# RWKV-7 block on one core: small matrix products handed to TensorE with more reckoned slack, the bonus product after its two parts, and parameter vectors transposed as soon as they are loaded

## The chip, the cores and the metric

The kernel runs on one core of a Trainium2 chip. The metric is the device time of one execution in microseconds (us). Three executions of the kernel before took 1826.38, 1829.63 and 1830.56 us; the median is 1829.63 us. One further execution was profiled. It took 1826.64 us, and its profile spans 1824.9 us from the first to the last instruction.

Names of the engines as the profile has them: PE is TensorE (matrix products; PEld is its loading of the stationary operand), DVE is VectorE, ACT is ScalarE, POOL is GpSimd, SP is SyncE, which only issues transfers here (SPq is its queue).

## What is computed

One layer of a decoder block in float32, 1024 positions of width 1024 (the two blocks of 512 positions are called b = 0 and b = 1 below):

```
h = rms_norm(x, norm_mix)
p = h @ w_in                      # 1024 x 5408: r k v | wd ad gd | conv b c x | gates a, b
p_rw = p_rw + (token_shift(p_rw) - p_rw) * mu_shift
out_a = rwkv7(r, k, v, wd, ad, gd, ...)        # 8 heads of 64
out_b = b * conv3(c * x_c)
x = x + (sigmoid(ga) * (out_a @ w_proj_a) + sigmoid(gb) * (out_b @ w_proj_b)) @ w_out_mix
x = x + cross_attention(rms_norm(x), rms_norm(mem))      # 4 heads, 256 memory tokens
x = x + relu(rms_norm(x) @ w_up)**2 @ w_down
y = rms_norm(x)
```

and within `rwkv7`, for each head and position t:

```
log_w = -softplus(-(w0 + tanh(wd) @ w_lora_w)) - 0.5;  decay = exp(-exp(log_w))
a = sigmoid(a0 + ad @ w_lora_a);  g = sigmoid(gd) @ w_lora_g
S_t = S_{t-1} diag(w_t) + (S_{t-1} a_t) b_t^T + v_t k_t^T;   y_t = S_t r_t
y   = group_norm(y) * ln_x_w + ln_x_b
y   = y + sum(r * k * r_k) * v                 # the bonus
out = y * g
```

## The kernel before

**Products in split form.** Every large float32 product is made of three passes over operands split in two parts: hi (the value rounded by ACT to the format that PE reads in one pass) and lo (the rest, subtracted by DVE or POOL). The weights are split on the chip as they come in (`wh`, `wl`), and so are the activations. One pass is a product of 128x128 by 128x512.

**Streams and a planner.** The program's order is not written out. Each piece of work is a Python generator (a stream); `Scheduler` keeps a reckoned time for each engine (`free`), a reckoned end of every write and read of a tile, and takes PE's reckoned time as "now". A stream yields the time from which it may go on. `need(t, ...)` is the reckoned end of the last write to these tiles plus 0.7 us; `pace("DVE")` is DVE's reckoned free time minus 0.3 us. `Scheduler.run` goes through the side streams in a fixed order of rank and takes the first that is ready; only when none is ready does the main stream (the large products) take its next step. So `need(x) + 0.7` in place of `need(x)` means: let PE's reckoned time pass by 0.7 us more, with products of the main stream in between, before this stream's next instructions are handed out. Each engine then works through its own list strictly in the order that came out, and waits at an instruction whose inputs are not there. The reckoned times decide the order alone; nothing of them is left in the program.

**Stages.** The main stream goes through the projections of `h` (`gemm` over `PROJ`: about 43 column tiles of `w_in`, each for both blocks), then the memory's keys and values (`mem_k`, `mem_v`: weights `w_kv`), `merge`, `w_out_mix`, attention, and the two MLP products. At the program's head `x_stage` turns x into the transposed `h` (PE transposes, ACT and DVE write hi and lo) for b = 0, then b = 1.

**RWKV as side streams beside the projections.** The state recurrence is done in 8 windows (pair of heads by block of 512 positions, `ORDER`), each in chunks of 64 positions:

- `lora_side`: the small products with `w_lora_*`, PSUM tag "c".
- `wkv_prepare(w)`: loads r, k, v, decay and a; DVE and ACT make the scaled operands `T1`, `BK`; then in this order on PSUM tag "s" (two banks, taken by `take_s`): sums of squares with `bd1` (128x2), the bonus sum with `bdo` (two passes, one over the hi and one over the lo part of `bs`), the values minus head mean with `cmat`, the chunk products `BK` by `T1` (`pss<-P,P`, 64 rows by 128 columns, two halves q of two banks h each), and two groups of transposes of `BK` (`pss<-ident,P`).
- `wkv_invert(w)`: POOL solves 32x32 triangles (`ex`), two 32x32 product groups follow.
- `wkv_chain(ws)`: for two windows at a time, 8 chunk steps of small products on tag "c" (`psc<-P,P`), with ACT and DVE copies in between.
- `wkv_out(w, a_)`: group norm of y, and the store to `d_y`.

In the profile nearly all instructions carry line 253, that of the recording helper; so the readings go by tiles. `P` is the ring of work tiles, `H` the ring that holds `h`, `wr` a raw weight tile, `st`, `sh`, `sm`, `ex` small rings, `psg`, `pss`, `psc`, `psy` the PSUM tags ("g" has three banks, "s" two, "c" two, "y" one).

Two details on which the change bears. In `wkv_prepare` the bonus stood as

```
yield need(tm_, bs)
split(bs[:, 0], bs[:, 1], sq)     # ACT makes hi, DVE makes lo
yield from take_s()
o = ps("s", [P, TB])
yield need(o)                     # looks at the PSUM bank alone
mm(o[:], cv["bdo"][:], bs[:, 0], True, False)
```

so nothing let the planner's time run until the two parts were reckoned written. And `constants()` waits until `r1` of block 0 is made (the row scale 1/rms), then transposes `vrow`, the 118 rows of small parameter vectors that SP loads with 16 small transfers behind the loads of x, into `vec`, by way of the one bank of tag "y". The main stream's first pair of jobs needs that bank for block 1.

Of the kernel before, what the change touches and what calls it, by code (L numbers as in the profile page):

```python
# [41 lines left out]
class Scheduler:  # L42
# [156 lines left out]
    def need(self, *tiles):  # L199
        return max(self.written(t) for t in tiles) + 0.7  # L200
# [58 lines left out]
def tile_hybrid_block(  # L259
# [74 lines left out]
    need, pace = sch.need, sch.pace  # L334
# [351 lines left out]
    def constants():  # L686
        yield until(("r1", 0))
        yield need(vrow)
        vps = ps("y", [P, P])
        yield need(vps)  # L690
        PE.transpose(vps[:], vrow[:], ident[:])
        yield need(vps)
        DVE.tensor_copy(vec[:], vps[:])
        cv["omu"] = derived("omu", "mu", -1.0, 1.0)
        cv["hw0"] = derived("hw0", "w0", 0.5)
# [52 lines left out]
    def until(*keys):  # L748
        return lambda: all(k in done for k in keys)
# [335 lines left out]
    def lora_side(name, parts, b, dst, fin):  # L1085
        yield until(("x", 1))
        for j in range(4):
            o2 = ps("c", [P, TB])
            yield need(o2) + 1.0
            cs = slice(j * P, (j + 1) * P)  # L1090
            for m, (lw, x_) in enumerate(parts):
                yield need(lw, x_)
                mm(o2[:], lw[:, cs], x_, m == 0, m == len(parts) - 1)
            yield need(o2)
            yield room
            z = sb("st", [P, TB])
            fin(z, o2, j)
            dma(dst[cs, blk(b)], z[:], (name, j, b))
# [121 lines left out]
    open_s = {"n": 0}  # L1220

    def take_s():

        yield lambda: open_s["n"] < BUFS["s"]
        open_s["n"] += 1
# [10 lines left out]
    def wkv_prepare(w):  # L1236
# [58 lines left out]
        o = ps("s", [P, 4, 2])  # L1295
        yield need(o)
        for q in range(4):
# [16 lines left out]
        split(bs[:, 0], bs[:, 1], sq)  # L1314

        yield from take_s()
# [13 lines left out]
        o = ps("s", [P, 4, 2, C])  # L1330
        yield need(o)
        for q in range(4):
# [26 lines left out]
        for q in range(2):  # L1359
            yield need(T1[0], T1[1], BK)  # L1360
            os_ = []
            for h in range(2):
                yield from take_s()
                o = ps("s", [P, 4, 2 * C])
                yield need(o)
                os_.append(o)
            for c in range(4):
                for h in range(2):
                    mm(os_[h][:, c, :], BK[HALF[h], 4 * q + c, :], T1[h][HALF[h], 4 * q + c, :])
            for h in range(2):  # L1370
                yield from evac_products(os_[h], q, h)
# [4 lines left out]
        for q in range(2):  # L1376
            yield from take_s()
            o = ps("s", [P, 4, P])
            yield need(o)
            for c in range(4):  # L1380
                PE.transpose(o[:, c, :], BK[:, 4 * q + c, :], ident[:])
            give_s()
            ACT.activation(BKt[:, 4 * q:4 * q + 4].rearrange("p c h k -> p c (h k)"), o[:], AF.Copy)
# [14 lines left out]
    def wkv_invert(w):  # L1398
# [35 lines left out]
        o = ps("s", [P, NCH, 32])  # L1434
        yield need(o)
        for c in range(NCH):
# [8 lines left out]
        o = ps("s", [P, NCH, 32])  # L1445
        yield need(o)
        for c in range(NCH):
# [7 lines left out]
    def wkv_chain(ws):  # L1455
# [16 lines left out]
        for c in range(NCH):  # L1472
            last = c == NCH - 1
            keep = not last or b == 0
            yield need(*[w["SV"] for w in ws])

# [18 lines left out]
            for h, H, i, w in HW:  # L1495
                if h == 0:
                    ACT.activation(w["SV"][H, c, h, :], o[H, 1, i], AF.Copy, scale=w["d2"][H, c:c + 1])
                else:
                    DVE.tensor_scalar(w["SV"][H, c, h, :], o[H, 1, i], w["d2"][H, c:c + 1], None, op0=ALU.mult)
            yield need(*[w["SV"] for w in ws])  # L1500
            if keep:
# [21 lines left out]
    def wkv_out(w, a_):  # L1523
# [9 lines left out]
        o = ps("s", [P, 4, 2])  # L1533
        yield need(o)
        for i in range(4):
# [9 lines left out]
        o = ps("s", [P, TB])  # L1545
        yield need(o)
        for i in range(4):
# [601 lines left out]
```

## Time and profile before

| | |
|---|---|
| executions | 1826.38, 1829.63, 1830.56 us, median 1829.63 |
| profiled execution | 1826.64 us, span 1824.9 us |
| busy, whole span | PE 96%, PEld 78%, DVE 59%, ACT 38%, POOL 28% |
| head, 0 to 60 us | PE 44.66 of 60 us busy |
| projections with RWKV, 100 to 600 us | PE 469.27 of 500 us busy, DVE 318.63, POOL 264.33, ACT 155.53 |
| end of RWKV, rest of the projections, 600 to 728 us | PE 59.12 of 60 and 68.00 of 68 us |
| memory keys and values, 728 to 775 us | PE 44.04 of 47 us |
| all after, 775 to 1825 us | PE 1031.40 of 1050 us |

How to read it: an interval of PE that is not busy is idle time "before" the instruction that ends it, and the profile names what released that instruction. A row of grouped instructions has the number of instructions, their busy time and mean duration in ns, and then the idle time of the engine just before them with the releasers. Consecutive products overlap in the records, so a product of 128x512 shows 389 ns while the next one starts about 227 ns later. PEclk is the share of full speed that TensorE's clock was granted.

### The profile page before, as it was taken

What the parts mean: (1) busy time and instruction counts of PE and PEld (TensorE: products, weight loads), DVE (VectorE), ACT (ScalarE), POOL (GpSimd) and SP (SyncE); (2) the same over time, 40 slices, a digit from 0 to 9 for tenths busy, and PEclk for the clock granted to TensorE, in tenths of its full rate; (3) what the DMA queues carried; (4) which work ended last, traced back from release to release, by engine and by line L of the source; (5) the groups of instructions that cost most, each with busy time, mean ns of one, the idle gap of its engine ahead of it and who ended that gap; (6) DMA issues with size and microseconds to landing.
All of it is one profiled execution on the core that took longest, in us unless ns stands there. A gap on an engine that the chain in (4) does not pass through costs nothing.

```text
span 1824.9 us, 26662 instructions
## 1 busy us (share of the span) xinstructions
PE 1756.1 (96%) x9914; PEld 1429.7 (78%) x9914; DVE 1078.5 (59%) x1694; ACT 698.2 (38%) x1233; POOL 518.3 (28%) x872
## 2 busy tenths in 40 slices
PE   7898999999989999999999999989999999999998
PEld 5677767767768788888888877868888888888887
DVE  4477665666754432455556765577767675654543
ACT  5623332123235332422333434354444444543542
POOL 3026653655545110000323433433233220000000
PEclk8999998999999999999999999999999999999999
DMA  6543532323435344744755668434454569765441
GB/s 215 207 125 91 155 93 76 93 82 104 108 86 153 116 139 135 217 162 166 229 179 164 203 190 260 134 102 158 157 178 144 173 196 352 259 213 193 159 118 55
DMA packets 303359, 289.19 MB, mean 158 GB/s; under 512 B 40744, under 2 KB 223134, under 8 KB 303230
## 3 DMA queue, kind: packets, MB, share of 16 engines
q1 hardware_dynamic: 302158, 286.97, 49.3%
q8 instruction: 78, 1.28, 0.3%
q10 hardware_dynamic: 1072, 0.53, 0.1%
q14 instruction: 51, 0.42, 0.1%
HBM read 193.06 MB, written 94.37 MB: 158 GB/s over the span
## 4 chain that ended last, share of the span: by engine, by line
PE 71%; DVE 8%; POOL 5%; issue 3%; DMA 3%; ACT 3%; SPq 0%; POOLq 0%; DVEq 0%; ACTq 0%
PE psg L253 47%; PE pss L253 12%; PE psc L253 9%; DVE P L253 4%; POOL ex L253 4%; PE psy L253 3%; DMA wr<-in_w_kv_dram 2%; ACT P L253 1%; DVE wl L253 1%; DVE st L253 1%; POOL P L253 1%; DVE sh L253 1%; ACT wh L253 1%; DMA P<-dn 0%; SPq L253 0%
## 5 line engine op out<-in xcount | busy, mean ns | idle before, releaser
L253 PE MATMUL psg<-H,wh 128*128 128x512 f32 x1808 | 583.5, 400 | 4.1 <-ACT H L253 1.8
L253 PEld LDWEIGHTS psg<-H,wh 128*128 128x128 f32 x1808 | 338.4, 190 | 75.8 <-ACT H L253 3.1
L253 PE MATMUL psg<-P,wh 128*128 128x512 f32 (+1 forms) x1240 | 371.0, 380 | 7.4 <-ACT P L253 3.0
L253 PE MATMUL psg<-H,wl 128*128 128x512 f32 x888 | 355.4, 400 | 0.0
L253 PEld LDWEIGHTS psg<-P,wh 128*128 128x128 f32 x1240 | 227.9, 188 | 51.7 <-ACT P L253 3.4
L253 PE MATMUL psg<-P,wl 128*128 128x512 f32 (+1 forms) x620 | 235.6, 380 | 0.0
L253 ACT ACTIVATE wh<-wr 128x1024 fp32r<-128x1024 f32 (+2 forms) x187 | 137.8, 764 | 244.3 <-PE psg L253 136.8
L253 DVE TENSOR_TENSOR wl<-wr,wh 128x1024 fp32r<-128x1024 f32 (+2 forms) x178 | 160.2, 923 | 91.4 <-ACT wh L253 90.5
L253 PEld LDWEIGHTS psg<-H,wl 128*128 128x128 f32 x888 | 168.7, 190 | 34.6 <-issue 0.2
L253 ACT ACTIVATE P<-P 128x512 fp32r<-128x512 f32 (+3 forms) x246 | 147.7, 634 | 79.3 <-DVE P L253 44.9
L253 DVE TENSOR_TENSOR P<-P,P 128x512 fp32r<-128x512 f32 (+2 forms) x204 | 146.6, 755 | 14.6 <-ACT P L253 13.2
L253 POOL TENSOR_TENSOR sm<-sm,mhalf 128x8 f32<-128x8 f32 (+2 forms) x18 | 22.8, 1267 | 413.9 <-DVE sm L253 413.9
L253 PEld LDWEIGHTS psg<-P,wl 128*128 128x128 f32 x620 | 116.8, 188 | 21.7 <-DVE wl L253 0.5
L253 POOL TENSOR_TENSOR ex<-ex,P 128x60 f32<-128x60 f32 (+24 forms) x248 | 94.8, 382 | 73.6 <-DMA P<-dn 58.1
L253 POOL TENSOR_TENSOR ex<-ex 128x60 f32<-128x60 f32 (+24 forms) x248 | 98.4, 397 | 19.4
L253 PE MATMUL pss<-P,wh 128*128 128x512 f32 x296 | 91.7, 390 | 1.1 <-DVE P L253 1.1
L253 DVE TENSOR_SCALAR P<-psc,sm 64x64 f32<-64x64 f32 x120 | 34.9, 291 | 88.9 <-ACT P L253 82.4
L253 ACT ACTIVATE P<-psc,sm 64x64 f32<-64x64 f32 (+1 forms) x128 | 42.5, 333 | 100.2 <-PE psc L253 60.1
L253 PE MATMUL psc<-P,P 128*64 128x64 f32 (+2 forms) x816 | 68.1, 252 | 10.3 <-DVE P L253 8.4
L253 DVE TENSOR_TENSOR P<-psg,P 128x512 f32<-128x512 f32 x44 | 30.3, 689 | 78.0 <-PE psg L253 73.7
L253 PEld LDWEIGHTS psc<-P,P 128*64 128x64 f32 (+2 forms) x816 | 46.4, 147 | 37.1 <-issue 15.4
L253 PE MATMUL psc<-P,wh 128*128 128x512 f32 x216 | 67.4, 394 | 0.0
(686 smaller groups left out, 2828.1 us busy)
## 6 DMA issues: line engine op xcount, KB each, us to landing
P<-d_t SPq DMA_DIRECT2D x56, 512.0 KB
wr<-in_w_in_dram SPq DMA_DIRECT2D x40, 512.0 KB
d_t<-P SPq DMA_DIRECT2D x64, 256.0 KB
d_x<-P SPq DMA_DIRECT2D x48, 256.0 KB
P<-d_x SPq DMA_DIRECT2D x24, 512.0 KB
d_t<-st SPq DMA_DIRECT2D x48, 256.0 KB
d_tg<-st SPq DMA_DIRECT2D x32, 256.0 KB
wr<-in_w_kv_dram SPq DMA_DIRECT2D x16, 512.0 KB
```

The lines of the kernel that those rows point to most:

```text
L253: return fn(*args, **kw)
```

## The change

All edits concern when the planner hands out work; no instruction is added or removed, and 8660 PE instructions stand in both programs.

- `constants()`: the transpose of `vrow` no longer waits for `r1`; it is handed out once the fourth tile of `h` of block 0 is made and `vrow`'s transfers are reckoned done, plus 1.0 us. The derived constants still wait for `r1`.
- `lora_side`: 1.5 us more before each of its products.
- `LATE = 0.7` us more before each group of small products of `wkv_prepare`, `wkv_invert` and `wkv_out` (in the chunk products also 1.4 us after the operands), 0.2 us at two points of each chain step.
- The bonus: `need(bs) + LATE` after the split, so that the two passes are handed out when both parts are reckoned written.

```diff
     def constants():
-        yield until(("r1", 0))
-        yield need(vrow)
+        yield until(("h", 0, 3))
+        yield need(vrow) + 1.0
         vps = ps("y", [P, P])
         yield need(vps)
         PE.transpose(vps[:], vrow[:], ident[:])
         yield need(vps)
         DVE.tensor_copy(vec[:], vps[:])
+        yield until(("r1", 0))
...
     def lora_side(name, parts, b, dst, fin):
...
             for m, (lw, x_) in enumerate(parts):
-                yield need(lw, x_)
+                yield need(lw, x_) + 1.5
                 mm(o2[:], lw[:, cs], x_, m == 0, m == len(parts) - 1)
...
+    LATE = 0.7
...
     def wkv_prepare(w):
...
         o = ps("s", [P, 4, 2])
-        yield need(o)
+        yield need(o) + LATE
         for q in range(4):
             mm(o[:, q, :], sq[:, q * P:(q + 1) * P], cv["bd1"][:])
...
         yield need(tm_, bs)
         split(bs[:, 0], bs[:, 1], sq)
-
+        yield need(bs) + LATE
         yield from take_s()
         o = ps("s", [P, TB])
         yield need(o)
...
         o = ps("s", [P, 4, 2, C])
-        yield need(o)
+        yield need(o) + LATE
         for q in range(4):
             mm(o[:, q], v[:, q * P:(q + 1) * P], cv["cmat"][:].rearrange("p h k -> p (h k)"))
...
         for q in range(2):
-            yield need(T1[0], T1[1], BK)
+            yield need(T1[0], T1[1], BK) + 2 * LATE
             os_ = []
             for h in range(2):
                 yield from take_s()
                 o = ps("s", [P, 4, 2 * C])
-                yield need(o)
+                yield need(o) + LATE
                 os_.append(o)
...
             o = ps("s", [P, 4, P])
-            yield need(o)
+            yield need(o) + LATE
             for c in range(4):
                 PE.transpose(o[:, c, :], BK[:, 4 * q + c, :], ident[:])
...
     def wkv_invert(w):
...
         o = ps("s", [P, NCH, 32])
-        yield need(o)
+        yield need(o) + LATE
...
     def wkv_chain(ws):
...
-            yield need(*[w["SV"] for w in ws])
+            yield need(*[w["SV"] for w in ws]) + 0.2
             o = ps("c", [P, 3, 2, C])
...
-            yield need(*[w["SV"] for w in ws])
+            yield need(*[w["SV"] for w in ws]) + 0.2
             if keep:
...
     def wkv_out(w, a_):
...
         o = ps("s", [P, 4, 2])
-        yield need(o)
+        yield need(o) + LATE
...
         o = ps("s", [P, TB])
-        yield need(o)
+        yield need(o) + LATE
```

What moves, at three places.

PE's list at the program's head: `psg` rows are the main stream's first two jobs for block 0 (`H` is `h`), `pss` and `psc` rows with `P_98` the transposes of x for block 1; `psy<-ident,st` is the transpose of the parameter vectors. Before, and then now:

```order
L253 MATMUL psg_196<-H_167,wh_188 128x512
L253 MATMUL psg_196<-H_175,wh_188 128x512
L253 MATMUL psg_196<-H_167,wl_189 128x512
L253 MATMUL psy_390<-ident,st_106 128x128
L253 MATMUL psg_398<-H_160,wh_186 128x512
```

```order
L253 MATMUL psg_196<-H_162,wh_188 128x512
L253 MATMUL psg_196<-H_170,wh_188 128x512
L253 MATMUL psy_281<-ident,st_106 128x128
L253 MATMUL psg_196<-H_162,wl_189 128x512
L253 MATMUL psg_195<-H_163,wh_186 128x512
L253 MATMUL psg_195<-H_171,wh_186 128x512
```

The transpose stood behind the last product of block 0 (eight tiles of `h`); it now stands within the third tile, ahead of five tiles' products and ahead of all transposes of block 1. On DVE the copy to `vec` moves with it: it stood behind the first tiles of block 1, and now stands ahead of the seventh tile of block 0 (`H_174`).

PE's list around the bonus product of the fourth window (`bdo`), in the first chain's time: `psc` and `psy` rows are chain products, `psg` the main stream. Before, and then now:

```order
L253 MATMUL psc_2563<-P_1039,P_914 64x64 x2
L253 MATMUL psc_2563<-P_1486,P_1282 64x64 x2
L253 MATMUL psg_2620<-H_160,wh_2369 128x512
L253 MATMUL psg_2620<-H_168,wh_2369 128x512
L253 MATMUL pss_2625<-P_2599,bdo 128x512 x2
L253 MATMUL psc_2631<-P_1039,P_912 64x64
```

```order
L253 MATMUL psg_2562<-H_167,wl_2333 128x512
L253 MATMUL psg_2690<-H_160,wh_2332 128x512
L253 MATMUL psg_2690<-H_168,wh_2332 128x512
L253 MATMUL psc_2644<-P_1056,P_914 64x64 x2
L253 MATMUL psc_2644<-P_1525,P_1302 64x64 x2
L253 MATMUL pss_2703<-P_2635,bdo 128x512 x2
L253 MATMUL psg_2690<-H_160,wl_2333 128x512
L253 MATMUL psg_2690<-H_161,wh_2332 128x512
```

Counted over the whole list, 754 products of the projections stood ahead of this bonus product, and now 778 do; five products of the projections now stand between it and the next chain step, where none stood.

SP's list where RWKV's last outputs (`sh<-d_y`, with the gate rows `sh<-d_g`) are loaded back for the merge, among stores of gate rows (`d_tg`) and loads of weights (`wr`). Before, and then now:

```order
L253 DMA sh_6572<-d_y 128x512
L253 DMA sh_6574<-d_g 128x512
L253 DMA d_tg<-st_6586 128x512
L253 DMA sh_6609<-d_y 128x512
L253 DMA sh_6611<-d_g 128x512
L253 DMA wr_6632<-in_w_in_dram 128x8x128
L253 DMA d_tg<-st_6625 128x512
L253 DMA d_tg<-st_6660 128x512
L253 DMA wr_6699<-in_w_kv_dram 128x8x128
L253 DMA d_tg<-st_6692 128x512
L253 DMA d_tg<-st_6724 128x512
L253 DMA wr_6763<-in_w_kv_dram 128x8x128
```

```order
L253 DMA d_y<-P_4981 128x512
L253 DMA wr_6673<-in_w_kv_dram 128x8x128
L253 DMA d_tg<-st_6666 128x512
L253 DMA sh_6692<-d_y 128x512
L253 DMA sh_6694<-d_g 128x512
L253 DMA d_tg<-st_6705 128x512
L253 DMA sh_6730<-d_y 128x512
L253 DMA sh_6732<-d_g 128x512
L253 DMA wr_6753<-in_w_kv_dram 128x8x128
L253 DMA d_tg<-st_6746 128x512
L253 DMA sh_6776<-d_y 128x512
L253 DMA sh_6778<-d_g 128x512
```

The first two `w_kv` loads stood behind all `d_y` loads; they now stand among the last three of them. RWKV's last products (the transposes in `wkv_out` of the eighth window) stood behind 1759 products of the projections and now stand behind 1883. From the product that PE started at 685.4 us in the profile before, PE's list is the same to the end.

More of the change, by code (lines that the diff above doesn't have):

```diff
@@ L1545, in wkv_out @@
         o = ps("s", [P, TB])
-        yield need(o)
+        yield need(o) + LATE
         for i in range(4):
```

## The prediction

> **What bounds the kernel now.** I read the busy shares first, then a table by stage, then who ended PE's idle time in the stage that the change touches, then that stage's PE groups with shapes kept apart.
>
> ```profile
> PE 1756.1 (96%) x9914; PEld 1429.7 (78%) x9914; DVE 1078.5 (59%) x1694; ACT 698.2 (38%) x1233; POOL 518.3 (28%) x872
> 100.00:600.00 500.00, 469.27 (x3578) 366.85 (x3578) 318.63 (x587) 155.53 (x304) 264.33 (x648) 0.97 0.38 106
> 600.00:660.00 60.00, 59.12 (x582) 43.22 (x580) 25.03 (x57) 25.25 (x59) 9.35 (x6) 1.00 0.30 89
> 728.00:775.00 47.00, 44.04 (x347) 42.12 (x346) 19.59 (x56) 22.59 (x69) 0.00 (x0) 1.00 0.72 220
> ```
>
> PE is the bound: 96% of the span. The second row and those below are stages: length, busy time of PE, PEld, DVE, ACT and POOL, granted clock, DMA share, GB/s. What small edits can win is PE's idle time and time at a lower clock. Between 100 and 600 us, where RWKV runs beside the projections, PE idles 500 - 469.3 = 30.7 us, and a clock of 0.97 is 0.03 x 500 = 15 us lost. So some 46 us is the ceiling there. DVE, the next engine, is 64% busy in it. Before 660 us the last chains leave PE hardly idle, and from the product at 685.4 us on PE's list does not change.
>
> ```profile
> PE pss L253 <- DVE P L253: 19.0, 19, 3.3
> PE psc L253 <- DVE P L253: 5.2, 9, 1.2
> PE pss L253 <- ACT P L253: 5.1, 4, 1.9
> L253 PE MATMUL pss<-P,P 64*128 64x128 f32 x256 | 27.0, 320 | 13.5 <-DVE P L253 13.2 <-POOL ex L253 0.3
> L253 PE MATMUL pss<-P,bdo 128*128 128x512 f32 x16 | 7.4, 473 | 9.0 <-ACT P L253 5.1 <-DVE P L253 3.8
> L253 PE MATMUL psc<-P,P 128*64 128x64 f32 x472 | 28.9, 243 | 5.4 <-DVE P L253 4.5
> L253 PE MATMUL pss<-ident,P 128*128 128x128 f32 x104 | 16.8, 276 | 2.2 <-DVE P L253 2.0
> L253 PE MATMUL psc<-P,P 128*128 128x512 f32 x24 | 7.7, 415 | 0.7 <-DVE P L253 0.7
> ```
>
> The first three rows are total idle us, times and longest; the others give idle time behind the second bar. All of it but a trace stands ahead of small products that were put into PE's list before DVE or ACT had their inputs: 13.5 + 9.0 + 5.4 + 2.2 + 0.7 = 30.8 us, the whole 30.7. None stands ahead of a large product (the `psg` rows of this stage have 0.0). So PE has other work at these points; it is only queued behind. The critical chain shows how fast that work goes:
>
> ```profile
> 657.64 42.42 PE psg L253 x187
> ```
>
> 42.42 / 187 = 0.227 us for a product of the main stream.
>
> **The change, part by part.** The profiled execution took 1826.6 us; the sum is made against it.
>
> *Bonus, 9.0 us in 8 windows.* One window in full:
>
> ```profile
> 156.71 0.40 PE L253 MATMUL pss<-P,bdo 128*128 128x512 f32 x1
> 157.88 0.80 DVE L253 TENSOR_TENSOR P<-P,P 128x512 fp32r<-128x512 f32 x1
> 158.73 0.50 PE L253 MATMUL pss<-P,bdo 128*128 128x512 f32 x1 [1.63 <-DVE P L253]
> ```
>
> The second pass waits until DVE has written the lo part. With the pass handed out when both parts are reckoned done and 0.7 us more, PE spends that time on main products instead: 1.63 us is seven of them. Bounds: all 9.0 us gone, or nothing if the wait moves on (below). I take 8.0, since two engines must be late by more than 0.7 us against the reckoning for a rest. **-8.0**.
>
> *Chunk products, 13.5 us.* Ten waits; five make nearly all of it:
>
> ```profile
> 167.83 0.58 PE L253 MATMUL pss<-P,P 64*128 64x128 f32 x2 [2.94 <-DVE P L253]
> 280.57 0.80 PE L253 MATMUL pss<-P,P 64*128 64x128 f32 x4 [1.78 <-DVE P L253]
> 354.08 0.38 PE L253 MATMUL pss<-P,P 64*128 64x128 f32 x2 [2.04 <-DVE P L253]
> 403.39 0.58 PE L253 MATMUL pss<-P,P 64*128 64x128 f32 x2 [1.77 <-DVE P L253]
> 525.99 0.47 PE L253 MATMUL pss<-P,P 64*128 64x128 f32 x2 [3.29 <-DVE P L253]
> ```
>
> They wait for the second PSUM bank, from which DVE is still copying the values product. Here only slack is added, 0.7 us on the bank (the 1.4 us on the operands counts only where these are last). The five lose 0.7 each, 3.5 us; the other five, 13.5 - 11.8 = 1.7 us together, go. That is 5.2. With 1.4 it would be 7.0 + 1.7 = 8.7; with a DVE that stays as far behind, 0. I take the lower of the two gains. **-5.2**.
>
> *Chain steps, 5.4 us.* 0.2 us at each of two points. The row above has nine waits of DVE in `psc`, one the 0.7 of `lora_side`; eight lose 0.2 each, 1.6, and what is below that, 5.4 - 4.5 = 0.9, goes. **-2.5**, between 0 and 5.4.
>
> *Transposes of `BK` and `lora_side`, 2.2 + 0.7 us.* Their waits are 0.7 us and less, the slack 0.7 and 1.5. **-2.4**, between 0 and 2.9.
>
> *The parameter vectors, at the head.* What goes is the wait of the bank of tag "y" for `vec`; what comes is a wait for the transfers:
>
> ```profile
> 18.41 0.39 PE L253 MATMUL psg<-H,wl 128*128 128x512 f32 x1
> 21.86 0.29 SPq L253 DMA_DIRECT2D st<-in_norm_final_dram  x1
> 22.03 0.30 PE L253 MATMUL pss<-ident,P 128*128 128x128 f32 x1 [0.72 <-issue]
> 23.33 0.30 PE L253 MATMUL pss<-ident,P 128*128 128x128 f32 x1 [1.00 <-DVE sm L253]
> 35.37 1.22 PE L253 MATMUL psy<-H,wh 128*128 128x512 f32 x2 [2.16 <-DVE vec L253]
> 0.79 0.58 ACTq L253 DMA_DIRECT2D st<-in_norm_mix_dram  x1
> 2.32 0.24 PE L253 MATMUL psy<-ident,st 8*128 8x8 f32 x1 [2.32 <-DMA st<-in_norm_mix_dram]
> ```
>
> The transpose now stands just ahead of the product that started at 18.41, but the last of the 16 small transfers is issued only at 21.86. The first transfer of this kind took from 0.79 to 2.32, 1.5 us, so the rows are there at about 23.4. PE stands still for 23.4 - 18.4 = 5.0 us, with all products of block 0 from the third tile on and all transposes of block 1 queued behind it, and DVE stands before the copy to `vec` with two tiles of `h` behind. 1.7 us (0.72 + 1.00) stood there anyway, since PE now finds those inputs ready; 2.16 goes later: 5.0 - 1.7 - 2.2 = +1.1. Block 1 pays or hides it:
>
> ```profile
> 43.74 0.69 ACT L253 ACTIVATE H<-pss,gmix 128x512 fp32r<-128x512 f32 x1 [5.68 <-PE pss L253]
> ```
>
> ACT idled 5.68 us for block 1's second transposes, which stood behind products of the main stream; they now stand ahead of most of these. Bounds: the two waits gone and nothing for it, -3.9, up to 5.0 and a slice of 3.4 us at half clock behind it, +6.7. I take the difference, **+1.1**.
>
> *Clock.* 15 us of clock went with 30.7 us idle. The slices in which it fell are those of the long waits:
>
> ```profile
> 280.00:300.00 20.00, 18.65 (x194) 14.20 (x194) 10.15 (x24) 5.32 (x16) 0.19 (x1) 0.83 0.22 50
> 400.00:420.00 20.00, 17.14 (x171) 12.76 (x166) 12.84 (x29) 5.21 (x15) 2.51 (x8) 0.83 0.13 22
> 440.00:460.00 20.00, 20.00 (x90) 16.55 (x89) 14.31 (x20) 3.55 (x5) 17.59 (x39) 1.00 0.53 157
> ```
>
> With 18.1 of 30.7 us idle gone, 59%, a proportional share is 8.9 us. But the long waits are shortened, not removed, so I take half, **-4.5**, between 0 and -15. The Trainium skill (TensorE: Matmul & The Clock Gate, Part 1: The HAM clock gate) has the clock fall to half after an idle window of about 3.4 us. Here it fell with no single wait above 3.3 us, so the trace shows it sooner than the page; by the page nothing here would depend on these waits and the term would be 0.
>
> *Waits that move on.* DVE gets no faster; where PE arrives earlier, the next small product may wait instead. I take a quarter of 18.1, **+4.5**, between 0 and 18.1.
>
> Sum: -8.0 - 5.2 - 2.5 - 2.4 + 1.1 - 4.5 + 4.5 = -17.0. That makes 1809.6 us of the profiled execution, which ran 3.0 us below the median; against the median **1812.6 us**.
>
> **Rivals.**
>
> 1. *The waits move on.* For it: five chunk products wait for DVE right after the bonus product, so DVE is late as a whole, not one input. Against it: every moved group has main products put ahead of it, and DVE is 64% busy. Bonus and chunk terms would be 0 and the clock would stay: -2.5 - 2.4 + 1.1 = -3.8, 1825.8 us.
> 2. *RWKV becomes late, slower.* Slack adds up along the windows. RWKV's last products move from behind 1759 to behind 1883 main products, 124 x 0.227 = 28 us later against the projections.
>
> ```profile
> 657.04 0.60 PE L253 MATMUL pss<-ident,P 128*128 128x128 f32 x4
> 673.61 0.32 SPq L253 DMA_DIRECT2D sh<-d_y  x1
> 679.79 0.32 SPq L253 DMA_DIRECT2D sh<-d_y  x1
> 692.74 0.38 SPq L253 DMA_DIRECT2D wr<-in_w_kv_dram  x1
> ```
>
> They ended at 657 and now stand where 685 was, 41 us ahead of the memory stage. SP takes the `d_y` loads 6.2 us apart, and three of them now stand among the `w_kv` loads, which had 12.9 us of room. If y came so late that these loads, 3 x 6.2 = 19 us, fell into the stage at 728, which already runs its DMA at 0.72 and waits for weights, each us would cost one. It decides from 13 us beyond the 28; for slower than before it takes 17 more. At 40 us beyond: 1812.6 + 27 = 1839.6 us. Against it: PE's order fixes the 28.
> 3. *The clock comes back in full*, 15 in place of 4.5: 1802.1 us. For it: a slice without idle time, 440 to 460 us, has 1.00. Against it: 12.6 us of waits stay, in the same places.
> 4. *The clock does not come back* (the page's rule; as a mechanism, the low slices have another cause, such as the sparse small products): 1817.1 us. For it: 280 to 300 us fell to 0.83 with only 1.35 us idle inside. Against it: all low slices lie in or just behind a slice with a long wait.
>
> **How the numbers follow.** Forecast 0.57, rival 1 0.17, rival 2 0.06, rival 3 0.10, rival 4 0.10. 0.2%, 3.7 us, is about what a measurement of this kernel can tell from no change: faster is below 1826.0. Forecast, rivals 3 and 4 and half of rival 1 are faster, 0.85; rival 2 and a little of rival 1 slower, 0.08; the rest is the same, 0.07. The range leaves out rival 2, the upper half of rival 1 and the tail of rival 3: 1799 to 1826. Its low end is the forecast with 8.7 in the chunk term, the full clock and no more than that; the likeliest one's own range is 1804 to 1822.
>
> **What would show it.** In the profile after: `pss<-P,bdo` with under 1 us of idle time; `pss<-P,P` 64*128 at about 8 and `psc<-P,P` 128*64 at about 3; PE busy some 483 of 500 us between 100 and 600, at 0.98; `psy<-ident,st` near 23.4 us with 5 us idle ahead of it and no wait for `vec`; the memory stage begun 17 us earlier. I am wrong if the bonus idle reappears ahead of `cmat` or chunk products, or if PE's time at 60 us is later by more than 3.

## The result and the profile after

| | before | after |
|---|---|---|
| executions, us | 1826.38 to 1833.60 (5), median 1829.63 | 1804.86 to 1810.48 (5), median **1807.4** |
| profiled execution | 1826.64, span 1824.9 | 1810.48, span 1808.8 |

The ratio is **0.9888**, 95% interval 0.9867 to 0.9909, so the change is clear of noise; the medians lie 22.2 us apart. The forecast of 1812.6 us is 5.2 us too high, inside its own range (1804 to 1822). The profiled execution of the change is its slowest of five; it lies 16.2 us under the profiled execution before (forecast: 17.0).

The profile after, in the views that the prediction used. First the busy line of the page, then the table by stage (start and end, length, busy us and instructions of PE, PEld, DVE, ACT and POOL, granted clock, DMA share, GB/s):

```profile
PE 1745.7 (97%) x9914; PEld 1423.7 (79%) x9914; DVE 1078.6 (60%) x1694; ACT 696.6 (39%) x1233; POOL 524.4 (29%) x872
```

```profile
0.00:60.00 60.00, 42.85 (x176) 32.95 (x177) 28.24 (x47) 34.28 (x68) 16.50 (x52) 0.90 0.65 215
100.00:600.00 500.00, 477.88 (x3631) 376.00 (x3630) 325.40 (x591) 158.18 (x308) 271.91 (x647) 0.99 0.38 108
711.00:758.00 47.00, 45.63 (x351) 43.61 (x351) 20.22 (x57) 24.14 (x72) 0.00 (x0) 1.00 0.75 230
```

PE idles 22.1 us between 100 and 600 us (30.7 before) and is granted 0.99 of its clock (0.97). The memory stage begins 18 us earlier (its first product at 704.8 us in place of 723.0), and PE idles 1.4 us in it (3.0).

The waits of that stage by releaser (total us, times, longest), then its groups, idle time behind the second bar:

```profile
PE pss L253 <- DVE P L253: 13.3, 13, 2.1
PE psc L253 <- DVE P L253: 5.4, 7, 1.1
```

```profile
L253 PE MATMUL pss<-P,bdo 128*128 128x512 f32 x16 | 5.6, 422 | 1.0 <-DVE P L253 1.0
L253 PE MATMUL pss<-P,P 64*128 64x128 f32 x256 | 23.7, 301 | 10.0 <-DVE P L253 10.0
L253 PE MATMUL psc<-P,P 128*64 128x64 f32 x472 | 27.7, 236 | 5.5 <-DVE P L253 5.4
L253 PE MATMUL pss<-ident,P 128*128 128x128 f32 x102 | 16.3, 275 | 3.5 <-DVE P L253 1.7 <-ACT P L253 1.6
L253 PE MATMUL pss<-P,P 32*32 32x32 f32 x448 | 10.5, 192 | 1.5 <-issue 0.8 <-DVE P L253 0.6
```

The bonus lost 8.0 of its 9.0 us, the chunk products 3.5 of 13.5. The chain steps kept theirs (5.4 before), the transposes gained 1.3 (2.2 before), and the 32x32 products of the inversion wait 1.5 us where they had waited for nothing.

The head, from the timeline of PE (start, length, the idle time and its releaser in brackets):

```profile
24.20 0.45 PE L253 MATMUL psy<-ident,st 128*128 128x128 f32 x1 [3.77 <-DMA st<-in_norm_final_dram]
56.70 0.76 PE L253 MATMUL psc<-P,P 128*128 128x512 f32 x1 [4.46 <-DVE P L253]
```

PE's 240th main product of the projections starts at 102.3 us (100.5 before); 0.8 us of the difference stands there already at the first main product, ahead of any change, so the head costs 1.0 us. It is not the stop for the vectors alone: up to there PE idles 2.7 us more than before, in which the second line above has a part (a product of `lora_side`, whose wait was 2.97 us before), and one cell less of half clock gives 1.7 us back. Comparing the start of the same products from there on: 18.2 us earlier at the end of the projections, 20.3 in the middle of the output product, 16.2 at the end. Behind the projections PE's list is the same in both, so the change is no reason for the last 4 us. They are 1.6 us more idle time and 1.7 us for one more time at half clock, which began at 1071.9 us, right behind a wait of 1.51 us that the kernel before has too (1.50 us, ended at 1090.3, with no half clock behind it). The other runs that have this part unaltered are 0.8 to 3.6 us longer in it than the kernel before, so it is rather the profiled execution before that was quick here.

Time at half clock between 60 and 690 us, summed from the records of the granted clock that begin there, fell from 27.3 us to 10.2. At half clock half of it is lost: 13.7 us before, 5.1 after. PE's idle time in the same stretch went from 32.0 to 24.3 us. Taken between the same two products instead, the 240th and the last of the projections, the 20.0 us by which they come closer are 9.3 us of idle time, 8.5 us of clock, and 2.2 us in the records themselves: from one product's start to the next, with waits and half clock left out, the bonus products take 4.3 us in place of 6.4 and the chunk products 20.9 in place of 22.1.

These are two single executions, and the one before was not a typical one. Each execution's mean granted clock is on record. Its span times what that clock lacks of 1 is its loss to the clock, over the whole span: 21.6 us on average for the kernel before (60 executions), 16.6 us for the change (10). So the clock gave 5.0 us, with a standard error of 1.0. The time without that loss fell from 1805.8 to 1790.9 us on average, so all the rest gave 14.9. The profiled execution before lost 25.5 us to the clock and took 1801.1 us without that loss. Its profile therefore shows too much of the one and too little of the other, and the split into groups, which profiles alone show, is unsure by some 5 us.

### The profile page after: what moved, and what is told of

It is laid out like the page before. It is cut to its first block, busy times and chain, and to the rows that moved or that the text cites. A ratio compares the mean times of both kernels' runs of the same rounds, so it can differ in the third digit from the quotient of the medians.

```text
span 1808.8 us, 26674 instructions
## 1 busy us (share of the span) xinstructions
PE 1745.7 (97%) x9914; PEld 1423.7 (79%) x9914; DVE 1078.6 (60%) x1694; ACT 696.6 (39%) x1233; POOL 524.4 (29%) x872
## 4 chain that ended last, share of the span: by engine, by line
PE 75%; DVE 8%; DMA 5%; POOL 4%; issue 3%; ACT 3%; SPq 1%; ACTq 0%; POOLq 0%; DVEq 0%
PE psg L253 50%; PE pss L253 12%; PE psc L253 9%; DVE P L253 4%; PE psy L253 4%; POOL ex L253 3%; ACT P L253 2%; SPq L253 1%; DVE wl L253 1%; DMA sh<-d_ob 1%; DVE st L253 1%; POOL P L253 1%; DVE sh L253 1%; ACT st L253 1%; DMA P<-dn 1%
## 5 line engine op out<-in xcount | busy, mean ns | idle before, releaser
L253 PEld LDWEIGHTS psg<-P,wl 128*128 128x128 f32 x620 | 116.8, 188 | 21.8 <-DVE wl L253 0.6
L253 DVE TENSOR_SCALAR P<-psc,sm 64x64 f32<-64x64 f32 x120 | 34.9, 291 | 77.9 <-ACT P L253 72.6
```

The lines of the kernel that those rows point to most:

```text
L253: return fn(*args, **kw)
```

## Experiments

Each ran beside the kernel before on one chip. "Idle" and "half clock" below are PE's idle us and the us lost at half clock between 60 and 690 us, worked out from the records of the profiled execution as above. "Last product" is the start of the profiled execution's last PE instruction against before (the change: -16.2). "Clock, all" and "rest, all" are means over all executions of a run, against those of the kernel before beside it: the loss to the clock over the whole span, and the time without that loss. They are sure to about 2 us and 1 us (standard errors).

| run | ratio (95%) | median us | clock, all | rest, all | idle | half clock | last product |
|---|---|---|---|---|---|---|---|
| before | 1 | 1825.75 to 1829.63 | 0 | 0 | 32.0 | 13.7 | 0 |
| the change, again | 0.9881 (0.9864 to 0.9899) | 1807.0 | -5.5 | -16.4 | 24.2 | 3.4 | -20.3 |
| bonus alone | 0.9970 (0.9958 to 0.9983) | 1819.67 | -2.6 | -3.9 | 28.7 | 6.8 | -9.8 |
| all but the bonus | 0.9996 (0.9981 to 1.0011) | 1826.49 | +2.3 | -3.5 | 33.8 | 13.7 | 0.1 |
| bonus and chunk slack | 0.9900 (0.9882 to 0.9917) | 1810.11 | 0.0 | -18.5 | 22.2 | 13.7 | -17.6 |
| change without chain slack | 0.9919 (0.9893 to 0.9945) | 1813.43 | +0.9 | -15.9 | 24.7 | 3.4 | -19.7 |
| change with old vectors | 0.9891 (0.9876 to 0.9907) | 1805.25 | -4.3 | -17.4 | 21.3 | 5.1 | -23.1 |
| change, LATE 1.4 | 0.9879 (0.9861 to 0.9897) | 1801.89 | -3.2 | -20.8 | 20.4 | 5.1 | -21.9 |
| old vectors, LATE 1.4 | 0.9825 (0.9802 to 0.9849) | 1797.59 | -5.6 | -26.4 | 17.3 | 1.7 | -29.0 |
| old vectors, LATE 2.8 | 0.9933 (0.9915 to 0.9952) | 1814.02 | -2.7 | -9.9 | 25.8 | 10.2 | -12.3 |
| old vectors, LATE 4.2 | 0.9983 (0.9970 to 0.9995) | 1823.02 | +6.1 | -9.5 | 21.8 | 8.5 | -6.1 |
| LATE 1.4, vectors 16 places later | 0.9816 (0.9791 to 0.9841) | 1792.76 | -8.6 | -25.2 | 19.5 | 3.4 | -34.9 |

The median of before differs between the chips and hours by 4 us, so runs of different groups are compared by ratios.

### Base for what follows: the change again

> The changed kernel unaltered, as the base for what runs beside it: a ratio of 0.987 to 0.991 to the kernel before, as in the comparison of the change.

0.9881. The result repeats.

### The bonus alone, and all but the bonus

```diff
 # bonus alone: before, with
         split(bs[:, 0], bs[:, 1], sq)
+        yield need(bs) + 0.7
         yield from take_s()
 # all but the bonus: the change, with
         split(bs[:, 0], bs[:, 1], sq)
-        yield need(bs) + LATE
         yield from take_s()
```

> The kernel before with the bonus wait alone (0.7 us after both parts). Theory A, each wait is its own late input: the idle time ahead of the bonus product goes from 9.0 to about 1, the chunk products keep their 13.5 us, and with the clock's share the time falls by 8 to 12 us, to 1818 to 1822 us; PE's idle time between 100 and 600 us is 22 to 23 us. Theory B, DVE is late as a whole and the waits move on: the chunk and cmat products behind it take what the bonus loses, idle time stays at 28 to 31 us and the time at 1826 to 1830 us.

> The changed kernel with the bonus handed out as before: slack and early vectors alone. Theory A: bonus idle time is back at 9 us, the chunk products have about 10, and the time is what is left of the gain, about 10 to 14 us less than before, 1816 to 1820 us. Theory B, the slack only moves waits and the bonus carries all of the gain: idle time between 100 and 600 us about 30 us, 1828 to 1832 us (the head's 1.8 us included).

The groups between 100 and 600 us, with the bonus alone and then with all but the bonus:

```profile
L253 PE MATMUL psc<-P,P 128*64 128x64 f32 x472 | 27.3, 233 | 9.1 <-DVE P L253 7.9
L253 PE MATMUL pss<-P,P 64*128 64x128 f32 x256 | 26.3, 304 | 10.7 <-DVE P L253 9.0 <-POOL ex L253 1.5
L253 PE MATMUL pss<-P,bdo 128*128 128x512 f32 x16 | 5.5, 408 | 1.2 <-DVE P L253 1.2
```

```profile
L253 PE MATMUL pss<-P,P 64*128 64x128 f32 x256 | 24.1, 305 | 7.0 <-DVE P L253 6.8
L253 PE MATMUL pss<-ident,P 128*128 128x128 f32 x92 | 14.4, 275 | 4.8 <-DVE P L253 4.1 <-ACT P L253 0.7
L253 PE MATMUL pss<-P,bdo 128*128 128x512 f32 x16 | 8.8, 550 | 12.8 <-DVE P L253 7.6 <-ACT P L253 5.1
```

The bonus alone comes between the two theories: its wait goes as theory A had it (7.8 us), the chunk products lose 2.8 us too, and of these 10.6 us 4.9 return, 3.7 of them in the chain steps (5.4 to 9.1). The time falls by 0.3%, some 3 to 8 us, less than theory A's 8 to 12. All but the bonus can't be told from before by its time: the chunk products lose 6.5 us, but the bonus product gains 3.8 (9.0 to 12.8) and the transposes gain 2.6. Over all its executions 3.5 us are gained beside the clock and 2.3 are lost to it. So on its own the slack does nearly what rival 1 says: it moves waits. The two edits alone are worth 0.30% and 0.04%, together 1.1 to 1.2%. They don't add, and which of them "carries" the gain has no answer: **the slack pays in full only once the bonus wait, which stood in its way, is gone.** All but the bonus has the early vectors in it, which cost some 1 to 3 us (below); the slack with neither was not run.

### Which slack: the chunk products' alone, and the chain's taken out

```diff
 # bonus and chunk slack: bonus alone, with
-            yield need(T1[0], T1[1], BK)
+            yield need(T1[0], T1[1], BK) + 2 * 0.7
...
-                yield need(o)
+                yield need(o) + 0.7
 # change without chain slack (both places)
-            yield need(*[w["SV"] for w in ws]) + 0.2
+            yield need(*[w["SV"] for w in ws])
```

> The kernel before with the bonus wait and the slack of the chunk products (1.4 us after the operands, 0.7 after each bank), nothing else. The bonus alone took 10 us off the profiled execution, all together 16 to 20. Theory A, the chunk slack is what works only once the bonus wait is gone: chunk idle time falls from 10.7 (bonus alone) to 6 to 8 us, the long waits that are followed by half clock go from four to two or less, ratio 0.989 to 0.992. Theory B, the rest of the slack (chain, bd1, cmat, transposes, inversion, output) is needed as well: 0.995 to 0.998, as with the bonus alone.

> The changed kernel without the 0.2 us at the two points of each chain step. Theory A, the chain slack does nothing (its idle time was 5.4 us before and 5.5 after): the time of the changed kernel within 2 us, chain idle time 5 to 6 us. Theory B, it holds back waits that would have grown, as they did with the bonus alone (9.1 us): chain idle time 8 to 9 us, the time 3 to 5 us above the changed kernel. Theory C, it costs: the time 2 to 4 us below.

The chunk products with the first, then the chain steps and the chunk products without the chain's slack:

```profile
L253 PE MATMUL pss<-P,P 64*128 64x128 f32 x256 | 22.3, 287 | 9.1 <-DVE P L253 6.4 <-POOL ex L253 2.7
```

```profile
L253 PE MATMUL psc<-P,P 128*64 128x64 f32 x492 | 28.1, 231 | 9.3 <-DVE P L253 8.1
L253 PE MATMUL pss<-P,P 64*128 64x128 f32 x256 | 21.7, 287 | 7.6 <-DVE P L253 5.2 <-POOL ex L253 2.1 <-POOL P L253 0.3
```

Bonus and chunk slack bring 0.990, some 18 of the 22 us, as theory A has it for the time. Its picture of why failed: chunk idle time fell by 1.6 us only (10.7 to 9.1), the chain steps lost more (9.1 to 4.1), and the clock gave nothing. Half clock stands in five places where the bonus alone had three, 13.7 us of loss for 6.8, and over all executions the clock loses as much as before (0.0), while the rest gains 18.5.

Without its slack the chain waits 9.3 us in place of 5.5, the 8 to 9 of theory B, and the median is 6.4 us above the change's beside it. The intervals overlap a little, and the profiled execution was the fastest of six, so the price is less sure than the wait. In that execution PE's idle time as a whole is the same with and without the chain's slack (24.2 and 24.7 us); over all executions too the rest is the same (-16.4 and -15.9), and what differs is the clock (-5.5 and +0.9). So the 0.2 us did not take away waits that stood there; they held back those that the other edits would have sent there, and what that is worth seems to lie in the clock.

### More slack

```diff
-    LATE = 0.7
+    LATE = 1.4        # and 2.8, 4.2
```

> The changed kernel with LATE at 1.4 us in place of 0.7. Theory A, a wait loses what is added to its slack: the chunk products' 10.0 us fall to about 6.5, the transposes' 3.5 to about 1.5, and with the clock the time falls by 5 to 8 us, to 1799 to 1803 us. Theory B, the waits move on: other small products take it, 1806 to 1809 us. Theory C, RWKV becomes late and the loads of its result fall among the memory weights: the memory stage (47 us before and after) grows, and the time is above 1811 us.

> Vectors transposed as before and LATE at 1.4 us. Theory A, the two act at different places and add: the 2 us of the head and the 4 us of the chunk products below the changed kernel, a ratio of 0.984 to 0.986, 1799 to 1802 us beside 1827 of the kernel before; PE's idle time from 60 to 690 us about 18 us (24.3 in the changed kernel, 20.4 with LATE 1.4 alone, 21.3 with the old vectors alone). Theory B, both end at the same floor: the same as either alone, 0.988.

> Vectors transposed as before and LATE at 2.8 us (1.4 gave a ratio of 0.9825). RWKV's last products stand behind 1979 main products (1759 before, 1883 in the change, 1923 with 1.4), 220 x 0.227 = 50 us later than before. Theory A, waits still lose what is added: chunk idle time from 5.9 to 2 to 4 us, one more us each in the transposes and the clock, 1793 to 1797 us. Theory B, rival 2 of the prediction with its own prices: 50 us is 9 beyond its point of 41, so up to 9 us come back in the memory stage, 1803 to 1807 us. Theory C, a floor is reached: the chain's and the lora products' waits remain, 1796 to 1800 us.

> As the run beside it with LATE at 4.2 us: RWKV's last products stand behind all 2048 main products that its window has, at least 289 x 0.227 = 66 us later than before. Theory B, rival 2: 25 us beyond its point of 41, so the loads of RWKV's result (3 x 6.2 = 19 us) fall into the memory stage and all of it is paid: 1810 us and more, PE idle in the memory stage above 10 us (3 before). Theory A, the loads are hidden there too: 1793 to 1800 us, PE idle in the memory stage 3 to 5 us.

"Old vectors" means that the parameter vectors are transposed as before the change. Chunk products at 1.4 us, with the new and with the old vectors:

```profile
L253 PE MATMUL pss<-P,P 64*128 64x128 f32 x256 | 21.9, 286 | 5.7 <-DVE P L253 3.9 <-POOL ex L253 1.6
```

```profile
L253 PE MATMUL pss<-P,P 64*128 64x128 f32 x256 | 22.0, 287 | 5.9 <-DVE P L253 5.9
```

At 1.4 us theory A holds for the waits: 10.0 us fell to 5.7 (expected 6.5), and with the old vectors the ratio went to 0.9825, more than expected. With the new vectors one product of `lora_side` waits 3.1 us and takes a part back; by its ratio this run can't be told from the change. At 2.8 that wait is 4.45 us, and weights are late in the memory stage. The timeline of PE:

```profile
183.74 1.65 PE L253 MATMUL psc<-P,P 128*128 128x512 f32 x3 [4.45 <-ACT st L253]
721.41 0.56 PE L253 MATMUL psg<-P,wh 128*128 128x256 f32 x2 [2.52 <-ACT wh L253]
723.91 0.58 PE L253 MATMUL psg<-P,wl 128*128 128x256 f32 x1 [1.94 <-DVE wl L253]
```

Half clock stands from 182.4 to 196.1 us beside the first of these. Against 1.4, PE loses 13.8 us between its 480th and 600th main product and 5.1 in the memory stage, 18.9 us, of which some 2 come back later: the last product is 16.8 us later. At 1814 us the run is slower than all three theories had it; none of them had the lora wait. At 4.2 RWKV is late. The timeline of PE, that of SP's queue, and the table of the stretch around them:

```profile
757.75 1.52 PE L253 MATMUL psg<-P,wh 128*128 128x512 f32 x2 [6.11 <-ACT P L253]
768.65 1.52 PE L253 MATMUL psg<-P,wh 128*128 128x512 f32 x2 [8.96 <-ACT P L253]
```

```profile
757.06 0.34 SPq L253 DMA_DIRECT2D sh<-d_y  x1
762.48 0.32 SPq L253 DMA_DIRECT2D sh<-d_y  x1
767.96 0.32 SPq L253 DMA_DIRECT2D sh<-d_y  x1
```

```profile
740.00:800.00 60.00, 44.93 (x212) 36.88 (x213) 27.50 (x45) 13.64 (x24) 7.48 (x6) 0.86 0.59 193
```

Three loads of RWKV's result come 5.4 us apart in the middle of `merge`, whose products wait 15.1 us for what is made of them. PE is 27.2 us ahead of before at the start of that stretch and 8.2 behind it: 19.0 us lost. The prediction's rival 2 had 3 x 6.2 = 19 us for three late loads. The figure agrees by luck: what is lost is the two waits, 15.1 us, and most of what is left is half clock, from 756.1 to 773.1 us. Rival 2 let the memory weights wait behind the loads; here it is the next stage that waits for the loads themselves.

### The parameter vectors

```diff
 # old vectors: constants() as before the change
-        yield until(("h", 0, 3))
-        yield need(vrow) + 1.0
+        yield until(("r1", 0))
+        yield need(vrow)
...
-        yield until(("r1", 0))
 # 16 places later in PE's list: the change with LATE = 1.4 and
-        yield until(("h", 0, 3))
+        yield until(("h", 0, 5))
```

> The changed kernel with the parameter vectors transposed as before, behind the row scale of block 0. Theory A, the stop of 3.8 us for the last small transfer costs 1 to 2 us of the whole: 1805.5 to 1806.5 us, PE at its 60th main product 1 to 3 us earlier. Theory B, the head's stop is paid back by block 1's earlier transposes: 1807 to 1808 us. Theory C, the early vectors gain by themselves, since the wait for the bank at 35 us returns: 1809 to 1811 us.

> LATE at 1.4 us, and the vectors transposed early but 16 places later in PE's list (behind the sixth tile of h, just behind block 1's first transposes, where PE was at 24.5 us with the old vectors; the last transfer landed at 24.2 in the change). Theory A, place alone decides: no wait for the transfers (3.8 us in the change) and none for the bank (2.7 us with the old vectors), so PE is 2 to 3 us earlier at its 240th main product than with the old vectors, and the ratio goes from 0.9825 to 0.981. Theory B, the head is paid for elsewhere: the wait moves to the transposes of block 1 and the ratio stays at 0.982 to 0.984. Theory C, the other order of the reckoned times behind it brings another long wait, as the 3.1 us of a lora product with LATE 1.4 and early vectors: 0.986 to 0.989, like that run.

By time, old and new vectors can't be told apart at LATE 0.7 (0.9891, 0.9888 and 0.9881). On PE's 240th main product they differ by 2.6 us in favour of the old ones, 1.1 of which stand there from the first product on; the 1.5 that are left are within the 1 to 3 of theory A (which named the 60th product; there it is 2.4). PE's timeline with the vectors 16 places later, and below it the wait for the bank with the old ones (LATE 1.4 in both):

```profile
24.63 0.30 PE L253 MATMUL pss<-ident,P 128*128 128x128 f32 x1 [1.00 <-DVE P L253]
25.07 0.30 PE L253 MATMUL psy<-ident,st 128*128 128x128 f32 x1
32.75 0.62 PE L253 MATMUL psy<-H,wh 128*128 128x512 f32 x2
```

```profile
35.21 0.73 PE L253 MATMUL psy<-H,wh 128*128 128x512 f32 x2 [2.72 <-DVE vec L253]
```

With the transpose behind the landing there is neither the wait for the transfers (3.77 us in the change) nor the one for the bank. PE is 4.6 us earlier at its 240th main product than with the old vectors, 2.3 at the end of the projections. The ratio of 0.9816 is the best of all, 0.65% under the change (the intervals are apart), though against 0.9825 the timing alone can't tell it, and so can't tell theory A from theory B. What it has over that run lies in the clock (-8.6 and -5.6 us), not in the rest (-25.2 and -26.4).

### What half clock hangs on

The change with 28 waits of graded length put into the first MLP product, where the kernel has none. Their products are not used.

```diff
+        def probes():
+            n = 0
+            for i in range(1, NP_ - 1):
+                for key in (("u", i, 0, 0), ("u", i, 1, 1)):
+                    yield until(key)
+                    yield pace("POOL")
+                    o = ps("y", [P, P])
+                    yield need(o)
+                    PE.transpose(o[:], probe[:], ident[:])
+                    for _ in range(REPS[n % len(REPS)]):
+                        POOL.memset(probe[:], 0.0)
+                    PE.transpose(o[:], probe[:], ident[:])
+                    n += 1
+        REPS = (2, 7, 3, 8, 4, 9, 5, 10, 6, 12, 14)
```

> The changed kernel with 28 waits put into the first MLP product, where PE has none: PE transposes a zero tile, POOL writes it again 2 to 14 times (0.21 us each), and PE transposes it again; the results are not used. So waits of about 0.6 to 3.2 us, some 8 us apart, at every phase. Theory A, the clock goes by cells of 3.41 us on a fixed grid, and a cell with about 1.5 us of idle time or more is followed by one at half clock: waits up to 1.3 us cost their own length, waits from 2.5 up cost 1.7 us more, those between do so when they lie in one cell. Theory B, only an idle time of a whole cell counts: none of the 28 is followed by a low clock, and the stage grows by the waits alone. Theory C, the clock falls with the share of idle time: low clock behind short waits too.

One execution, 1895.41 us. The waits came out at 0.59 to 4.09 us, 58.9 us in all. Every stretch of half clock begins on a grid of 3.413 us (the starts differ by whole multiples of it) and lasts one or two cells. Three waits from PE's timeline, and the table by cells of the grid around them (the column behind POOL is the granted clock):

```profile
1218.30 0.33 PE L253 MATMUL psy<-ident,probe 128*128 128x128 f32 x1 [2.41 <-POOL probe L253]
1360.10 0.33 PE L253 MATMUL psy<-ident,probe 128*128 128x128 f32 x1 [1.95 <-POOL probe L253]
1385.05 0.33 PE L253 MATMUL psy<-ident,probe 128*128 128x128 f32 x1 [2.21 <-POOL probe L253]
```

```profile
1214.00:1217.40 3.40, 1.88 (x9) 1.27 (x7) 3.22 (x4) 2.23 (x5) 3.23 (x6) 1.00 0.20 77
1217.40:1220.80 3.40, 2.50 (x12) 2.09 (x13) 3.37 (x7) 2.10 (x3) 0.67 (x4) 1.00 0.02 5
1220.80:1224.20 3.40, 3.40 (x17) 2.82 (x16) 2.43 (x4) 0.83 (x2) 0.00 (x0) 1.00 0.80 309
1357.30:1360.70 3.40, 1.45 (x8) 0.95 (x7) 0.00 (x0) 1.11 (x2) 1.43 (x7) 1.00 0.95 304
1360.80:1364.20 3.40, 3.40 (x10) 2.66 (x9) 0.00 (x0) 0.00 (x0) 0.00 (x0) 0.51 0.43 154
1381.20:1384.60 3.40, 1.63 (x8) 1.07 (x6) 0.32 (x1) 1.11 (x2) 1.30 (x7) 1.00 0.96 277
1384.60:1388.00 3.40, 2.96 (x14) 2.46 (x15) 0.00 (x0) 0.24 (x1) 0.33 (x2) 1.00 0.28 100
```

The wait of 2.41 us falls into two cells, 1.5 and 0.9 us idle, and nothing follows. The shorter one of 1.95 us lies in one cell, and the next cell runs at half clock: 10 instructions of PE in it, where the full cell at 1220.8 has 17. The third leaves 1.8 us in its first cell: nothing follows. Over the stage, of the cells at full clock, 25 had 0.5 to 1.81 us idle and none was followed by half clock; of two with 1.87 us one was; all ten from 1.95 us up were. Theory A holds, with a sharper edge than expected and a higher one (1.87 against 1.5). From the last product ahead of the first wait to the products behind the last one, the stage took 357.0 us, against 265.4 for the same products in the change: 91.5 us more. 58.9 are the waits themselves, the 44.4 us at half clock account for 22.2, and the 56 added transposes take 10.1 from their start to the next product's. That is 91.2, so half of the time at half clock is the price.

## Why the prediction was right

The terms are read from the two profiled executions, as the prediction had them.

*Bonus, -8.0.* Measured -8.0 (9.0 to 1.0). But in the run with it alone nearly half of what went (4.9 of 10.6 us) returned elsewhere.

*Chunk products, -5.2.* Measured -3.5. The working, 0.7 us off each of five waits and the five short ones gone, took the row of before as fixed. The waits moved and changed their number. Doubling the slack did take 4.3 more, near the 3.5 by which the working goes from 5.2 to 8.7.

*Chain, -2.5, and transposes and `lora_side`, -2.4.* These terms failed: 0.1 and 1.3 us more idle time in place of 4.9 less. The step that failed is to reckon each group's slack against its own wait of before. When the bonus and chunk waits ended, these groups came next. The chain's slack was spent on waits that did not stand in the old profile (9.3 us without it), which no row of before could show.

*Waits that move on, +4.5.* Too small: idle time between 100 and 600 us fell by 8.6 us, where the terms without it gave 18.1. So 9.5 us moved on between these two executions, half and not a quarter.

*Clock, -4.5.* The size held: -5.0 over all executions (21.6 to 16.6 us), -5.5 in the repeat. The two profiles have -8.6 and -10.3, since the profiled execution before lost more than the average one. The working did not hold. The prediction took a share of the idle time and halved it, since the long waits were only shortened. It is not a share: bonus and chunk slack gained 18.5 us beside the clock, and nothing from it. Shortening a wait of 2 or 3 us by 0.7 to 1.5 can bring its cell of the clock's grid under the edge, and then the whole cell of 3.41 us, 1.7 us of loss, goes. Before, the cells followed by half clock in this stage had 1.6 to 3.25 us idle. How many of these cells go is a matter of where the waits fall, so half a share was a guess that came out.

*Parameter vectors, +1.1.* Measured +1.0 by the 240th product against before, +1.5 against the run with the old vectors. The wait was 3.77 us in place of 5.0, the landing at 24.2 in place of 23.4, and there is no wait for `vec` any more. Block 1's second transposes still keep ACT waiting (5.73 us, 5.68 before). That +1.0 fits so well is in part luck, for it holds waits of `lora_side` and a gain of the clock that the term did not have. PE is not late at 60 us: at the main product where PE stood then before, it is 0.8 us early.

*Rivals.* Rival 1 is what happens with the slack alone and half of what happens in the change. Rival 2 did not happen at 28 us of lateness, may begin to show at 50 (LATE 2.8, 5.1 us in the memory stage), and took 19 at 66 us or more. The room that the prediction gave it was a little large: from the place at 685.4 us to the memory stage's first product at 723.0 it is 38 us, not 41. Rival 3 did not happen: over all executions 5.0 us of its 15 came back, though in the profile of the second run, between 60 and 690 us, 10.3 of 13.7 did. Rival 4, the clock does not come back, is out for this change, but describes bonus and chunk slack, where some 18 us were gained with nothing from the clock. What spoke for it, the low clock with 1.35 us idle between 280 and 300 us, follows a cell that began at 277.0 and had 1.6 us idle. Its mechanism, sparse small products, does occur (last section).

In the two profiled executions the total fits (16.2 for 17.0 us) because two errors cancel: 5.0 us too much from idle time (13.6 forecast, 8.6 measured) and 4 too little from the clock. Over all executions the clock's term fits (5.0 for 4.5), and the rest gave 14.9 us, 16.4 in the repeat, where 12.5 were forecast. So waits turned into work, as predicted, and by more than predicted; which groups have the 2 to 4 us above the forecast stays open, since only one execution of the kernel before was profiled.

## What to carry to other kernels

When several small waits stand one behind another in a strictly ordered list, each edit's worth depends on the others: here the bonus alone gave 0.3%, the slack alone next to nothing, both 1.1 to 1.2%. Try such edits together, and grade the slack: 1.4 us gave more than 0.7, while at 2.8 and 4.2 other products waited, and most of the gain was lost. Among this kernel's dense products, a wait that leaves more than about 1.9 us idle in one cell of the clock's grid costs its own length plus 1.7 us, and more where the cell behind it is thinly filled too (last section). And one profile is one execution: where the clock moves by several us from one to the next, compare its mean over many before a gain is split into idle time and clock.

## What was not expected of the hardware

The clock's edge. The Trainium skill (TensorE: Matmul & The Clock Gate, Part 1: The HAM clock gate) gives a free-running window of 3413 ns, which the grid of these runs shows, and has the clock fall after an idle window of about 3.4 us. The runs disagree with the second: in dense products an idle time of 1.95 us in a cell of 3.41 was enough every time, and 1.81 never was. In the stage with RWKV's small products, over the 13 other profiles, half clock followed all 18 full-clock cells with more than 1.9 us idle, 16 of 28 with 1.4 to 1.9, two of the 460 with less, and two with no idle time at all. One of these two is the cell from 304.4 to 307.8 us with the bonus alone. PE's timeline there:

```profile
304.57 1.84 PE L253 MATMUL pss<-bd,P 128*128 128x2 f32 x16
306.68 0.69 PE L253 MATMUL pss<-P,P 32*32 32x32 f32 x32
```

PE is busy, but with products of 2 and 32 columns. So idle time only stands in for what PE streams. Count the columns of the products that start in a cell (512 for one of 128x512, 2 for one of 128x2; a cell full of main products has 15 of them, 7680 columns). Then one edge fits both stages. From 60 to 1780 us in all 14 profiles, half clock followed all 50 full-clock cells with under 2560 columns, 19 of 24 with 2560 to 2816, two of the 79 with up to 3700, and none of the 6783 with more. The same count tells how long half clock stays: of 44 half-clock cells with up to 3328 columns 32 were followed by another, of 60 with more none. The 4.45 us wait was followed by four half-clock cells (2560, 3200, 2944 and 3456 columns), of which only the last is over 3328; the 3.29 us wait of the kernel before by one (3584). That the columns themselves are what counts is not shown; no run varied them alone.
